# Value products of two attentions with 64 columns of one head, even and odd key blocks in the two column halves of TensorE

## The chip, the cores and the metric

The kernel runs on one core of one Trainium2 chip. A core has five engines with an instruction stream each: TensorE (PE in the profile, its weight loads PEld), VectorE (DVE), ScalarE (ACT), GpSimd (POOL) and SyncE (SP, which here only issues DMAs). They meet through semaphores. The working memory is SBUF; TensorE writes its products to PSUM, from which VectorE or ScalarE must take them. Both memories have 128 partitions. The metric is the device time of one execution in microseconds, the median of the runs.

## What is computed

One layer of a diffusion transformer for 512 latent positions and 256 context positions of width 1024. Four mixers work side by side on slices of one input projection, and their outputs are concatenated, projected by `w_out`, and passed to a mixture of 16 experts (two per position). The change touches the last product of two of the mixers, the differential attention (A) and the neighbourhood attention (B):

```python
# A: 4 heads, 2 x 32 query/key channels, 64 value channels, 768 keys (256 context + 512 latent)
s = jnp.einsum('bqhcd,bkhcd->bhcqk', q, k) * (A_QK ** -0.5)
p = jax.nn.softmax(s, axis=-1)
a = p[:, :, 0] - lam * p[:, :, 1]
o = jnp.einsum('bhqk,bkhd->bqhd', a, v)          # then an rms norm over the 64 channels of a head
# B: 4 heads of 64 channels, keys in a window of rows and columns, and the 256 context keys
p = jax.nn.softmax(jnp.concatenate([s_win, s_ctx], axis=-1), axis=-1)
ol = jnp.einsum('brqhik,brikhd->brqhd', p_win, v_rows) + jnp.einsum('brqhk,bkhd->brqhd', p_ctx, vc)
# afterwards
xl = xl + g1_l * (jnp.concatenate([a_l, b_l, p_l, h_l], axis=-1) @ lp['w_out'])
```

## The kernel before

The work goes through stages: modulation vectors (`ada`), the input projection in pieces, pool mixer and hyena convolution, then the two attentions, `w_out` with the residual (`xl`), the router, the experts, and a last norm. Each engine's instructions are ordered ahead of time by a scheduler that simulates the program; on the chip each engine keeps that order. A tile is taken from a pool under a tag with a fixed number of buffers, and an instruction that writes a new tile waits until the readers of the tile that had the buffer before are done.

Attention A (`attnA`) has 16 tiles of 128 queries, one for each of 4 heads and 4 query blocks. For a tile, TensorE makes two score rows `s` (L755, L756), VectorE takes each row's minimum (L773, scores have the opposite sign), ScalarE the exponentials `eA` (L774), and L783 and L784 join the two softmaxes. Two tiles later `outp` transposes the result on TensorE (`tA`, L801) and copies it to `aT` (L802), 6 key blocks of 128 by 256 queries for a pair of tiles. `av` then makes the value product for that head and pair (8 times in all): 6 matmuls with 128 value columns, which are those of two heads, accumulate into `poA` (L762), and ScalarE copies the 64 rows of the head that is wanted into `oA` (L764). After two heads a norm follows: `msA` (L815) on TensorE, and on VectorE four reciprocals L818, then L819 and L820.

The other generator, `projB` followed by `attnB`, is woven into A. `projB` makes the inputs of attention B (`pn` and `pl`, matmuls of L75 to L77: a product of values that are split in a high and a low part is three matmuls, and L71 and L72 make such a split, `wh` and `wl` for weights, `mix` for mixer outputs). It ends at about 301 us of the span, where the first scores `sB` of B are made. `attnB` has 16 tiles too, transposes `tB` (L993, copied to `eT` by L994), and 8 value products `poB`: 2 matmuls over 256 queries for the context (L1001) and 4 over 128 queries for the window (L1006), copied to `oB` by L1009. In the same stretch the modulation for the gate `g1` is made (`ad`, L416, with 32 columns), and the weights of `w_out` are multiplied by it (L452) and split (L71, L72). `w_out` itself is `pw` (L75 to L77), 24 halves of which L1047 adds to `xl`; the first two of four mixer groups come from B, so some of its matmuls stand among B's tiles and the rest behind.

The PSUM tag "x" has two buffers (`xbank`): in this stretch `tA`, `poA`, `msA` and `poB` and the columns of the modulation take turns in them. `tB` and `sB` use another tag.

```python
def xbank(name, shape=(128, 512)):
    return psx.tile(list(shape), F32, tag="x", name=name, bufs=2)
```

A float32 matmul appears as two instructions in the trace, and as one row in the order lists below; matmuls of split values (fp32r) are one in both.

Of the kernel before, what the change touches and what calls it, by code (L numbers as in the profile page):

```python
# [46 lines left out]
def tile_hybrid_block(ctx, tc, ins, out):  # L47
# [684 lines left out]

    LAG = 2

    def attnA():
        avs = aw([128, 6, 256], F32, "av")
        SY.dma_start(avs, avd.rearrange("(j p) c -> p j c", p=128))
        tiles = [(h, qt) for h in range(4) for qt in range(4)]
        qk, ss, st = {}, {}, {}
# [19 lines left out]
        def av(h, qp, aT):  # L759
            po = xbank("poA", (128, 256))  # L760
            for c in range(6):
                T.matmul(po, avs[:, c, (h // 2) * 128:(h // 2 + 1) * 128], aT[:, c, :], start=(c == 0), stop=(c == 5))  # L762
            rr = slice((h % 2) * 64, (h % 2) * 64 + 64)
            A.copy(st["os"][rr, qp * 256:(qp + 1) * 256], po[rr, :])  # L764

        def soft(ti, h, qt):
            if qt == 0 and h + 1 < 4:
# [141 lines left out]
    def attnB():  # L909
# [55 lines left out]
        for ti, (h, qt) in enumerate(tiles):  # L965
            if qt == LQ and h + 1 < 4:
                load_bias(h + 1)
            if ti == LT:
                load(1)
            if qt == 0 and h % 2 == 0:  # L970
                st["os"] = o1 if h == 0 else bw([128, 512], F32, "oB", 2)
            _, _, bv, bvx = ld[h // 2]
            bias = ld["b", h]
            p = sB.pop((h, qt))
            e = bw([128, 512], F32, "eB", NEB)
            ml = cst.tile([128, 4], F32, tag="ml", name="ml", bufs=6)
            V.tensor_sub(e[:, :256], p[:, :256], bias[:, qt, :])
            A.copy(e[:, 256:], p[:, 256:])
            V.tensor_reduce(ml[:, 0:1], e, axis=AX.X, op=ALU.min)
            A.activation(e, e, AF.Exp, scale=-1.0, bias=ml[:, 0:1], accum_out=ml[:, 1:2])  # L980
            V.reciprocal(ml[:, 1:2], ml[:, 1:2])
            A.activation(e, e, AF.Copy, scale=ml[:, 1:2])
            yield 1
            if ti + 2 < 16:
                scores(*tiles[ti + 2])
            yield 1
            qq = qt % 2
            if qq == 0:
                st["eT"] = e1 if ti == 0 else bw([128, 4, 256], F32, "eT", NET)
            eT = st["eT"]  # L990
            p = xbank("tB")
            for i in range(4):
                T.transpose(p[:, i * 128:(i + 1) * 128], e[:, i * 128:(i + 1) * 128], ident)  # L993
            (A.copy if ti % 2 else V.tensor_copy)(eT[:, :, qq * 128:qq * 128 + 128],  # L994
                                                  p.rearrange("p (c q) -> p c q", q=128))
            if qq == 1:
                yield 1
                qp = qt // 2
                po = xbank("poB", (128, 256))
                for i in range(2):  # L1000
                    T.matmul(po, bv[:, 4 + i, :], eT[:, 2 + i, :], start=(i == 0), stop=False)  # L1001
                for q2 in range(2):
                    qt_ = qp * 2 + q2
                    for i in range(2):
                        vv_ = bv[:, (0 if qt_ == 0 else 2) + i, :] if qt_ in (0, 3) else bvx[:, qt_ - 1 + i, :]
                        T.matmul(po[:, q2 * 128:(q2 + 1) * 128], vv_, eT[:, i, q2 * 128:(q2 + 1) * 128], start=False,  # L1006
                                 stop=(q2 == 1 and i == 1))
                rr = slice((h % 2) * 64, (h % 2) * 64 + 64)
                A.copy(st["os"][rr, qp * 256:(qp + 1) * 256], po[rr, :])  # L1009
            if qt == 3 and h % 2 == 1:  # L1010
                put_mix(None, 2 + h // 2, st["os"])
        flush()
# [981 lines left out]
```

## Time and profile before

| | |
|---|---|
| median of 3 runs | 752.04 us (747.57 to 754.37) |
| profiled execution | 753.25 us, of which 750.9 us are the span |
| mean granted TensorE clock in it | 0.945 of full speed |
| TensorE busy | 657.6 us (88%), 3886 matmul instructions |
| VectorE busy | 366.7 us (49%) |
| ScalarE busy | 245.4 us (33%) |

The span runs from the first to the last recorded instruction; 2.35 us lie around it. Busy shares are means over stages that are bound by different things, so the stretch in which the two attentions stand, from 240 to 421 us of the span, is read by itself. An instruction of TensorE overlaps the next in the trace, so the cost of one is read from the distance of two starts; the chain of waits gives such distances.

### The profile page before, as it was taken

The numbers are of one execution on the slowest core, as the hardware profiler recorded it, in microseconds if no ns is written. First come the engines' busy times: TensorE is split into PE (matmuls) and PEld (weight loads), VectorE is DVE, ScalarE is ACT, GpSimd is POOL, SyncE is SP. The second block draws the span as 40 slices with busy tenths as digits, with TensorE's granted clock in tenths as the row PEclk, the third lists the DMA queues.
The fourth block names the chain that finished last, engine by engine and source line by source line (L and its number), as shares of the span: only waits on it lengthen the run. The fifth ranks groups of instructions, "written<-read, shape, count | busy, mean of one in ns | idle before, by whom it ended". The sixth has DMA issues, their size and how long they took to land.

```text
span 750.9 us, 10264 instructions
## 1 busy us (share of the span) xinstructions
PE 657.6 (88%) x3886; PEld 421.5 (56%) x3886; DVE 366.7 (49%) x664; ACT 245.4 (33%) x421; POOL 145.0 (19%) x135
## 2 busy tenths in 40 slices
PE   3879999999879999689899947999999999976791
PEld 1457777879767796477788734444434445321230
DVE  3699835777816776994644673101111122211036
ACT  3573414341226774876831431000100001000024
POOL 1027433222205300000000351010211222111102
PEclk9969999999989999969999976999999999998995
DMA  8972357674483582595611675999789999999983
GB/s 318 417 260 110 127 189 263 267 263 159 152 219 140 172 273 71 175 389 195 244 57 57 239 281 214 413 412 406 276 282 321 375 405 376 407 394 399 394 314 116
DMA packets 46242, 197.81 MB, mean 263 GB/s; under 512 B 6330, under 2 KB 12961, under 8 KB 29290
## 3 DMA queue, kind: packets, MB, share of 16 engines
q1 hardware_dynamic: 38250, 175.55, 61.9%
q0 software_dynamic: 7056, 18.11, 8.4%
q10 hardware_dynamic: 880, 3.42, 1.1%
q8 instruction: 33, 0.54, 0.3%
q14 instruction: 23, 0.19, 0.1%
HBM read 177.79 MB, written 21.25 MB: 265 GB/s over the span
## 4 chain that ended last, share of the span: by engine, by line
PE 53%; DMA 10%; DVE 9%; ACT 4%; issue 3%; SPq 0%; POOL 0%; ACTq 0%; DVEq 0%; POOLq 0%
PE h L1449 16%; DMA mw<-in_moe_w_dram 8%; PE y L1516 7%; PE poA L762 3%; PE y L1502 2%; PE pw L75 2%; PE pw L76 2%; PE pw L77 2%; PE pn L76 2%; PE pn L77 1%; DMA qst<-qd 1%; PE pn L75 1%; DVE wl L72 1%; PE tpx L1413 1%; PE ad L416 1%
## 5 line engine op out<-in xcount | busy, mean ns | idle before, releaser
L1449 PE MATMUL h<-mw,xT 128*32 128x256 f32 (+2 forms) x928 | 154.7, 487 | 10.7 <-DMA mw<-in_moe_w_dram 10.6
L1449 PEld LDWEIGHTS h<-mw,xT 128*32 128x32 f32 (+2 forms) x928 | 55.9, 129 | 99.0 <-issue 66.7
L1464 ACT ACTIVATE hs<-h 64x512 f32<-64x512 f32 (+2 forms) x21 | 10.8, 512 | 195.7 <-PE h L1449 154.2
L1516 PE MATMUL y<-mw,hx 128*32 128x256 f32 (+2 forms) x432 | 70.1, 478 | 1.9 <-ACT hx L1476 0.7
L75 PE MATMUL pl<-ht,wh 128*128 128x512 f32 x128 | 52.6, 411 | 3.8 <-DVE bk L72 2.5
L77 PE MATMUL pl<-ht,wl 128*128 128x512 f32 x128 | 52.1, 407 | 0.0
L76 PE MATMUL pl<-ht,wh 128*128 128x512 f32 x128 | 52.0, 406 | 0.0
L1531 POOL DMA_INDIRECT xld<-ysb,r_ids x16 | 25.0, 1564 | 115.2 <-DVE ysb L1528 75.1
L1516 PEld LDWEIGHTS y<-mw,hx 128*32 128x32 f32 (+2 forms) x432 | 25.6, 127 | 34.4 <-issue 27.0
L1465 DVE SCALAR_TENSOR_TENSOR hs<-hs,r_gsl,h 64x512 f32<-64x512 f32 (+1 forms) x13 | 9.7, 744 | 67.0 <-ACT hs L1464 44.9
L72 DVE TENSOR_TENSOR wl<-raw,wh 128x2048 fp32r<-128x2048 f32 x14 | 33.4, 2388 | 13.9 <-ACT wh L71 13.9
L773 DVE TENSOR_REDUCE ml<-s 128x1 f32<-128x768 f32 x32 | 30.3, 948 | 12.7 <-PE s L756 12.6
L774 ACT ACTIVATE eA<-s,ml 128x768 f32<-128x768 f32 x32 | 28.8, 902 | 18.1 <-DVE ml L773 13.9
L71 ACT CAST wh<-raw 128x2048 fp32r<-128x2048 f32 x14 | 26.7, 1910 | 19.7 <-DMA raw<-in_w_in_dram 17.3
L75 PEld LDWEIGHTS pl<-ht,wh 128*128 128x128 f32 x128 | 24.6, 192 | 10.2 <-DVE bk L72 2.7
L1335 POOL DMA_INDIRECT xg<-hld,r_ids x12 | 12.2, 1015 | 85.3 <-PE tpx L1413 72.8
L762 PE MATMUL poA<-aT,av 128*128 128x256 f32 x96 | 26.8, 431 | 2.1 <-DVE aT L802 1.3
L76 PEld LDWEIGHTS pl<-ht,wh 128*128 128x128 f32 x128 | 24.5, 191 | 6.9 <-issue 1.6
L77 PEld LDWEIGHTS pl<-ht,wl 128*128 128x128 f32 x128 | 24.4, 191 | 6.4 <-issue 1.3
L1047 DVE TENSOR_TENSOR xl<-pw,xl 128x512 f32<-128x512 f32 x24 | 16.4, 688 | 20.3 <-PE pw L77 20.0
L75 PE MATMUL pw<-wh,mix 128*128 128x512 f32 x64 | 26.1, 407 | 0.0
L1414 DVE COPY xT<-tpx 128x512 f32<-128x512 f32 (+3 forms) x12 | 7.2, 602 | 37.9 <-PE tpx L1413 37.8
(453 smaller groups left out, 1419.2 us busy)
## 6 DMA issues: line engine op xcount, KB each, us to landing
mw<-in_moe_w_dram SPq DMA_DIRECT2D x92, 1024.0 KB
raw<-in_ada_dram SPq DMA_DIRECT2D x24, 1024.0 KB
raw<-in_w_in_dram SPq DMA_DIRECT2D x10, 1024.0 KB
raw<-in_w_out_dram SPq DMA_DIRECT2D x4, 1024.0 KB
mw<-in_moe_w_dram SPq DMA_DIRECT2D x6, 512.0 KB
mixd<-mx SPq DMA_DIRECT2D x5, 512.0 KB
kst<-kd SPq DMA_DIRECT2D x24, 96.0 KB
xin<-in_x_dram SPq DMA_DIRECT2D x4, 512.0 KB
```

Of the source, the lines that this page charges most:

```text
L71: A.copy(hi, src)
L72: (eng or V).tensor_sub(lo, src, f(hi))
L75: T.matmul(ps, a[0], b[0], start=start, stop=False)
L76: T.matmul(ps, a[0], b[1], start=False, stop=False)
L77: T.matmul(ps, a[1], b[0], start=False, stop=stop)
L762: T.matmul(po, avs[:, c, (h // 2) * 128:(h // 2 + 1) * 128], aT[:, c, :], start=(c == 0), stop=(c == 5))
L773: V.tensor_reduce(ml[:, cmp:cmp + 1], s[:, 0:768], axis=AX.X, op=ALU.min)
L774: A.activation(e[:, cmp, :], s[:, 0:768], AF.Exp, scale=-1.0, bias=ml[:, cmp:cmp + 1], accum_out=ml[:, 2 + cmp:3 + cmp])
L1047: V.tensor_add(xv, p, xv)
L1449: T.matmul(p, xk, b, start=(k == 0), stop=(k == 7))
L1516: T.matmul(p, x[k], b, start=(k == 0), stop=(k == 3))
L1531: G.indirect_dma_start(out=dst_, out_offset=bass.IndirectOffsetOnAxis(ap=at_, axis=0), in_=y, in_offset=None, bounds_check=last_, oob_is_e ...
```

## The change

Each value product uses only the 64 value columns of the head that is wanted. Even key blocks write partitions 0 to 63 of the PSUM tile, odd key blocks partitions 64 to 127, so that each half of the tile collects half of the sum. The number of matmuls is the same, each with 64 columns in place of 128. The halves are then added: a new function `halves_sum` lets ScalarE copy one half to the destination in SBUF, and VectorE adds the other half to it. In place of 16 copies of ScalarE there are 16 copies and 16 additions.

```diff
@@ -732,6 +732,13 @@
 
     LAG = 2
 
+    def halves_sum(dst, h, qp, po):
+
+        o = (h % 2) * 64
+        d = dst[o:o + 64, qp * 256:(qp + 1) * 256]
+        A.copy(d, po[64 - o:128 - o, :])
+        V.tensor_add(d, po[o:o + 64, :], d)
+
     def attnA():
         avs = aw([128, 6, 256], F32, "av")
         SY.dma_start(avs, avd.rearrange("(j p) c -> p j c", p=128))
@@ -759,9 +766,9 @@
         def av(h, qp, aT):
             po = xbank("poA", (128, 256))
             for c in range(6):
-                T.matmul(po, avs[:, c, (h // 2) * 128:(h // 2 + 1) * 128], aT[:, c, :], start=(c == 0), stop=(c == 5))
-            rr = slice((h % 2) * 64, (h % 2) * 64 + 64)
-            A.copy(st["os"][rr, qp * 256:(qp + 1) * 256], po[rr, :])
+                q = c % 2 * 64
+                T.matmul(po[q:q + 64], avs[:, c, h * 64:(h + 1) * 64], aT[:, c, :], start=(c < 2), stop=(c >= 4))
+            halves_sum(st["os"], h, qp, po)
 
         def soft(ti, h, qt):
             if qt == 0 and h + 1 < 4:
@@ -997,16 +1004,16 @@
                 yield 1
                 qp = qt // 2
                 po = xbank("poB", (128, 256))
+                hc = slice((h % 2) * 64, (h % 2) * 64 + 64)
                 for i in range(2):
-                    T.matmul(po, bv[:, 4 + i, :], eT[:, 2 + i, :], start=(i == 0), stop=False)
+                    T.matmul(po[i * 64:i * 64 + 64], bv[:, 4 + i, hc], eT[:, 2 + i, :], start=True, stop=False)
                 for q2 in range(2):
                     qt_ = qp * 2 + q2
                     for i in range(2):
-                        vv_ = bv[:, (0 if qt_ == 0 else 2) + i, :] if qt_ in (0, 3) else bvx[:, qt_ - 1 + i, :]
-                        T.matmul(po[:, q2 * 128:(q2 + 1) * 128], vv_, eT[:, i, q2 * 128:(q2 + 1) * 128], start=False,
-                                 stop=(q2 == 1 and i == 1))
-                rr = slice((h % 2) * 64, (h % 2) * 64 + 64)
-                A.copy(st["os"][rr, qp * 256:(qp + 1) * 256], po[rr, :])
+                        vv_ = bv[:, (0 if qt_ == 0 else 2) + i, hc] if qt_ in (0, 3) else bvx[:, qt_ - 1 + i, hc]
+                        T.matmul(po[i * 64:i * 64 + 64, q2 * 128:(q2 + 1) * 128], vv_, eT[:, i, q2 * 128:(q2 + 1) * 128],
+                                 start=False, stop=(q2 == 1))
+                halves_sum(st["os"], h, qp, po)
             if qt == 3 and h % 2 == 1:
                 put_mix(None, 2 + h // 2, st["os"])
         flush()
```

The lines behind the new function are 7 higher in the changed kernel: `s` is L762 and L763 there, `poA` L770, the row minimum L780, the join L791, `tA` L808, `msA` L822, `poB` L1009 and L1014; the new copy is L739 and the new addition L740.

The scheduler orders the engines anew, and the order moves at more places than the edited lines. TensorE at the first value product of A, before:

```order
L762 MATMUL poA<-aT,av 128x256 x6
L755 MATMUL s<-kst,qst 128x512
L756 MATMUL s<-kst,qst 128x256
L801 MATMUL tA<-ca,eA 128x128 x4
L755 MATMUL s<-kst,qst 128x512
L756 MATMUL s<-kst,qst 128x256
L75 MATMUL pn<-wh,ht_338 128x256 x2
L801 MATMUL tA<-ca,eA 128x128 x2
```

and in the changed kernel:

```order
L770 MATMUL poA<-aT,av 64x256 x6
L762 MATMUL s<-kst,qst 128x512
L763 MATMUL s<-kst,qst 128x256
L808 MATMUL tA<-ca,eA 128x128 x4
L762 MATMUL s<-kst,qst 128x512
L763 MATMUL s<-kst,qst 128x256
L75 MATMUL pn<-wh,ht_338 128x256 x2
L762 MATMUL s<-kst,qst 128x512
L763 MATMUL s<-kst,qst 128x256
```

The two transposes `tA`, which use the tag "x", stood before the last pair of scores here; they now stand behind it, behind 19 more `pn` and behind another pair of scores. VectorE at the same place, before:

```order
L773 TENSOR_REDUCE ml<-s 128x1
L72 TENSOR_TENSOR wl<-raw,wh 128x2048
L773 TENSOR_REDUCE ml<-s 128x1
L784 SCALAR_TENSOR_TENSOR eA<-eA,ml 128x768
L802 COPY aT<-tA 128x2x128
```

and in the changed kernel:

```order
L780 TENSOR_REDUCE ml<-s 128x1 x2
L72 TENSOR_TENSOR wl<-raw,wh 128x2048
L740 TENSOR_TENSOR oA<-poA,oA 64x256
L791 SCALAR_TENSOR_TENSOR eA<-eA,ml 128x768
L780 TENSOR_REDUCE ml<-s 128x1
```

The addition stands directly behind the split `wl` of a weight block; the row minimum that stood behind that split stands ahead of it now, and the copy `aT` has left this place.

TensorE at the end of the projection of B, where the last `pl` and the first scores `sB` stand; before (14 more `pl`, with one group of transposes among them, follow these rows, then `sB`):

```order
L75 MATMUL pl<-ht_338,wh 128x512
L755 MATMUL s<-kst,qst 128x512
L756 MATMUL s<-kst,qst 128x256
L76 MATMUL pl<-ht_340,wh 128x512
L815 MATMUL msA<-oA_2465,ca 128x512
L416 MATMUL ad_2516<-raw,sl_145 32x512
L755 MATMUL s<-kst,qst 128x512
L756 MATMUL s<-kst,qst 128x256
L416 MATMUL ad_2516<-raw,sl_145 32x512 x7
L77 MATMUL pl<-ht_338,wl 128x512
L75 MATMUL pl<-ht_338,wh 128x512
```

and in the changed kernel, from the last two `pl` on:

```order
L76 MATMUL pl<-ht_341,wh 128x512
L77 MATMUL pl<-ht_339,wl 128x512
L75 MATMUL sB<-bk_1994,bq_2756 128x256
L76 MATMUL sB<-bk_1994,bq_2756 128x256
L77 MATMUL sB<-bk_1994,bq_2756 128x256
L75 MATMUL sB<-bk_1994,bq_2756 128x256
L76 MATMUL sB<-bk_1994,bq_2756 128x256
L77 MATMUL sB<-bk_1994,bq_2756 128x256
L770 MATMUL poA<-aT,av 64x256 x3
L762 MATMUL s<-kst,qst 128x512
L763 MATMUL s<-kst,qst 128x256
L770 MATMUL poA<-aT,av 64x256
```

Of the 32 pairs of score rows of A, 24 stand before the last `pl` in the kernel before and 20 in the changed one; of the value products of A four and three; `msA` and the `ad` of the `g1` gate have moved behind the last `pl` (`msA` is 14 rows behind the last of these, and eight `ad` follow it).

TensorE at the last value product of B; before (13 more `pw` follow these rows, and then the six that use the last `oB`):

```order
L76 MATMUL pw<-wl,mix_2839 128x512
L1001 MATMUL poB<-eT,bv 128x256 x2
L1006 MATMUL poB<-eT,bvx 128x128 x2
L1006 MATMUL poB<-eT,bv 128x128 x2
L77 MATMUL pw<-wh,mix_2839 128x512
L75 MATMUL pw<-wh,mix_2838 128x512
L76 MATMUL pw<-wl,mix_2838 128x512
L77 MATMUL pw<-wh,mix_2838 128x512
L75 MATMUL pw<-wh,mix_2838 128x512
L76 MATMUL pw<-wl,mix_2838 128x512
```

and in the changed kernel:

```order
L77 MATMUL pw<-wh,mix_2845 128x512
L1009 MATMUL poB<-eT,bv 64x256 x2
L1014 MATMUL poB<-eT,bvx 64x128 x2
L1014 MATMUL poB<-eT,bv 64x128 x2
L75 MATMUL pw<-wh,mix_2845 128x512
L76 MATMUL pw<-wl,mix_2845 128x512
L75 MATMUL pw<-wh,mix_2845 128x512
L76 MATMUL pw<-wl,mix_2845 128x512
L77 MATMUL pw<-wh,mix_2845 128x512 x2
```

The `pw` that don't need the last `oB` stood behind the last value product and have moved before it; the six that do follow it directly. On VectorE the eight additions of B stand one to each value product, the last of them directly before the L72 that splits the last `oB`.

## Rows read from the trace of the kernel before

**Rows 1.** The page: shares of the chain that ended last, by engine.
```profile
PE 53%; DMA 10%; DVE 9%; ACT 4%; issue 3%; SPq 0%; POOL 0%; ACTq 0%; DVEq 0%; POOLq 0%
```

**Rows 2.** Windows: time, then PE, PEld, DVE, ACT, POOL busy, PEclk, DMA share, GB/s.
```profile
240.00:301.00 61.00, 58.39 (x358) 46.96 (x356) 43.87 (x68) 40.21 (x69) 10.96 (x7) 1.00 0.55 185
301.00:348.00 47.00, 37.46 (x174) 30.04 (x173) 38.72 (x63) 34.95 (x68) 0.77 (x1) 0.82 0.72 265
348.00:369.00 21.00, 18.01 (x117) 14.91 (x116) 13.15 (x28) 16.51 (x36) 0.00 (x0) 1.00 0.74 295
369.00:421.00 52.00, 52.00 (x263) 43.39 (x261) 23.75 (x38) 16.44 (x29) 0.00 (x0) 1.00 0.20 69
```

**Rows 3.** Timeline of PE at a value product of A (start, duration, instruction).
```profile
255.76 1.89 PE L762 MATMUL poA<-aT,av 128*128 128x256 f32 x8
...
258.70 0.60 PE L801 MATMUL tA<-ca,eA 128*128 128x128 f32 x4
```

**Rows 4.** Timeline of PE around matmuls with 32 columns.
```profile
261.57 0.28 PE L756 MATMUL s<-kst,qst 96*128 96x256 f32 x1
261.78 1.92 PE L416 MATMUL ad<-raw,sl 128*32 128x512 f32 x16
...
263.86 0.28 PE L76 MATMUL pn<-wl,ht 128*128 128x256 f32 x1
```

**Rows 5.** Timeline of PE in the experts: 64 and 128 columns.
```profile
577.01 3.65 PE L1516 MATMUL y<-mw,hx 128*64 128x512 f32 x16
...
583.76 3.70 PE L1516 MATMUL y<-mw,hx 128*128 128x512 f32 x8 [0.75 <-ACT hx L1476]
```

**Rows 6.** The chain of waits, 301 to 350 us (start, length, what).
```profile
304.60 2.20 DVE raw L452
...
321.23 5.33 PE poA L762 x12
...
337.18 4.00 PE poA L762 x12
...
345.74 2.59 PE poA L762 x12
348.33 0.86 PE poB L1001 x4
349.19 0.89 PE poB L1006 x8
```

**Rows 7.** DVE by line, 301 to 348 us: busy, mean ns, idle before.
```profile
L452 DVE TENSOR_TENSOR raw<-raw,g1b 128x2048 f32<-128x2048 f32 x4 | 9.1, 2282 | 1.9 <-issue 1.9
L773 DVE TENSOR_REDUCE ml<-s 128x1 f32<-128x768 f32 x8 | 7.5, 944 | 0.6 <-PE s L756 0.6
L784 DVE SCALAR_TENSOR_TENSOR eA<-eA,ml 128x768 f32<-128x768 f32 x5 | 5.0, 1008 | 0.1
...
L72 DVE TENSOR_TENSOR wl<-raw,wh 128x2048 fp32r<-128x2048 f32 x2 | 4.6, 2279 | 0.0
L802 DVE COPY aT<-tA 128x256 f32<-128x256 f32 x8 | 3.3, 413 | 4.0 <-PE tA L801 4.0
L977 DVE TENSOR_TENSOR eB<-sB,bias 128x256 f32<-128x256 f32 x7 | 2.8, 415 | 0.4 <-PE tB L993 0.4
```

**Rows 8.** DVE by line, 285 to 304 us.
```profile
L818 DVE RECIPROCAL oA<-oA 128x128 f32<-128x128 f32 x4 | 3.4, 909 | 0.9 <-ACT oA L816 0.9
```

**Rows 9.** Timeline at the last value product of B.
```profile
415.59 0.37 ACT L1009 COPY oB<-poB 64x256 f32<-64x256 f32 x1 [6.25 <-PE poB L1006]
...
415.99 0.63 ACT L71 CAST mix<-oB 128x512 fp32r<-128x512 f32 x1
...
416.65 0.69 DVE L72 TENSOR_TENSOR mix<-oB,mix 128x512 fp32r<-128x512 f32 x1
...
419.83 0.40 PE L75 MATMUL pw<-wh,mix 128*128 128x512 f32 x1
```

**Rows 10.** Windows in the experts, columns as in rows 2.
```profile
640.00:660.00 20.00, 19.35 (x210) 7.93 (x208) 4.50 (x11) 1.56 (x3) 3.11 (x2) 1.00 1.03 401
```

## The prediction

> **What bounds the kernel now.** The page comes first: TensorE makes 53% of the chain that ended last, VectorE 9% [rows 1]. That is a mean, so the stretch of the change is read next, in windows [rows 2]. From 240 to 301 us TensorE is busy for 58.4 of 61.0 us: the projection of B bounds it. From 301 to 348 us it is busy for 37.5 of 47.0 us, at a granted clock of 0.82, and VectorE for 38.7: here VectorE is the fullest engine. From 348 to 369 us it is mixed, and from 369 to 421 us TensorE has no gap at all. The chain shows how the second stretch is made: pieces of VectorE, such as the 2.20 us of L452, take turns with three value products of A, which take 5.33, 4.00 and 2.59 us for the same 12 instructions [rows 6]. The reader is to see two things: the same saved matmul time is worth all of itself in the first and last stretch, and in the second only where a value product is what VectorE waits for. Behind 421 us router and experts follow from the end of `w_out`, and where the experts run on the weights' DMAs there is no slack to give time back (TensorE 19.35 of 20 us, DMA share 1.03 [rows 10]); I let them move as one block.
>
> **The matmuls.** A value product of A takes 2.59 us [rows 6], 12 instructions of 0.216 us. Two instructions with 64 columns in the two halves run side by side: in the experts 16 with 64 columns take 3.65 us where 8 with 128 columns take 3.70 [rows 5]. So a product of A falls to 1.30 and saves 1.30, eight times 10.4 us. One of B takes 0.86 us for L1001 and 0.89 for the eight instructions of L1006, 1.75 together [rows 6]; halved it saves 0.87, eight times 7.0. Gross 17.4 us. What rows 5 leave open is the weight load: there 512 columns follow each load, here 256 and in L1006 only 128. For L1006 the bounds are therefore 0.44 and 0.89 as now; I take 0.44, from the only rows with 64 columns. With 0.89 the seven products of B on the path would give 3.1 us less.
>
> The Trainium skill, "TensorEngine Tiling (Array Packing)", section Tile-to-Partition Mapping (Restrictions), says that column tiling disables the fast weight load. That speaks against this change where few columns follow a load; no row here shows such a product, and by the rule alone the sum below would be at its upper bound for L1006.
>
> **Going in and out of column halves.** The 32-column `ad` shows what a visit costs. From the score matmul ahead of it to the second matmul behind it 2.29 us pass (261.57 to 263.86 [rows 4]). The work in it is 16 instructions of 512 columns, four side by side, as much as 8 of 256 full columns, 8 x 0.216 = 1.73, and two fp32r matmuls of 256 columns, 0.12 each. (A pair of score rows has 768 columns: 258.70 - 255.76 - 2.59 = 0.35 us [rows 3], 0.12 for 256.) That leaves 2.29 - 1.73 - 0.23 = 0.33 us for a visit. In the new order score rows split some products of A, so that there are 20 visits: 6.6 us. The bounds are nothing, if 64 columns behave as the 128-column visit of rows 3 that fits without a remainder, and 0.33. I take 0.33, since `ad` is the row of the same kind. Net on TensorE: 17.4 - 6.6 = 10.8 us.
>
> The Trainium skill, "TensorEngine Tiling (Array Packing)", section Tiling Modes (Key Properties), says that a change of the tiling mode drains TensorE. It gives no duration. The trace agrees, with the 0.33 us of rows 4; without such a cost the net would be the gross 17.4.
>
> **The copy and the addition.** ScalarE's copies stay 16, 0.37 us each [rows 9]. VectorE gets 16 additions. No row has a 64 x 256 one; the nearest is L977, PSUM and SBUF, 128 x 256: 0.415 us [rows 7]. As VectorE's time is by elements of a partition, I take 0.41 for each, 6.6 us in all, of which five fall into the second stretch (2.0 us), where VectorE is the fullest. The buffer of tag "x" is now held past the copy to the end of the addition, and that addition stands in VectorE's queue behind other work: at the first product of A behind a `wl` of 2.28 us [rows 7]. What needs the buffer are the next transposes `tA`; the scheduler has put them 23 rows later, behind scores and `pn`, so TensorE has work meanwhile. If that cover were gone, TensorE would wait for the `wl` and the addition, 2.7 us.
>
> **The first stretch, and what leaves it.** In the new order four pairs of score rows, one product of A, `ad`, `msA` and a few transposes have moved from before the last `pl` to behind it. By rows: 4 x 0.35 = 1.4, 2.6, 2.1 (rows 4 with its visit), some 0.9 for `msA` with two instructions of 512 columns (4 x 0.216), and 0.4: 7.4 us. The three products that stay save 3 x 1.30 = 3.9 and pay four visits, 1.3. The projection ends 7.4 + 2.6 = 10.0 us earlier.
>
> **The second stretch, and what comes into it.** Four pairs are two tiles of A. On VectorE a tile is two row minima (0.944 each), a join (1.008) and a copy (0.413) [rows 7], 3.3 us, twice 6.6. The reciprocals L818 of the first norm, which stood beside the projection, come along: 4 x 0.909 = 3.6 [rows 8]. With the five additions it is 12.2 us. That is the lower end, if the new work fills VectorE's gaps. The upper end goes by whole tiles: the stretch's 47.0 us less the four L452 (9.1) and two `wl` (4.6), which don't grow, for four tiles: 33.3 / 4 = 8.3 a tile, 16.7 for two. Against it stand the three products on the chain, 5.33 + 4.00 + 2.59 = 11.9, halved: 6.0. So A ends between 12.2 - 10.0 - 6.0 = -3.8 and 16.7 - 16.0 = +0.7. At the busy share that VectorE has there (38.72 / 47.0 = 0.82) the 12.2 become 14.9, which gives **-1.1**; I take that.
>
> The Trainium skill, "TensorEngine Tiling (Array Packing)", section Performance Considerations (PSUM Bottleneck), warns that tiling speeds TensorE and not the emptying of PSUM. It speaks for the upper end; by it alone the sum of this stretch would be +0.7. The trace so far agrees as far as VectorE's 0.82 goes.
>
> **The third and the last stretch.** A product of B on the chain saves 0.87 - 0.33 = 0.54. Three stand on it before 369 us, -1.6, and four behind, where TensorE has no gap, -2.2. At the last one cover is lost. Before, 19 `pw` followed it on TensorE, up to 419.83 us; in that time copy, cast and split of `oB` (415.59, 415.99, 416.65 [rows 9]) were done. In the new order these `pw` stand ahead of the product and the six that need `oB` directly behind it. TensorE waits for copy 0.37, addition 0.41, cast 0.63 and their hand-offs, 0.1 each: **+1.7**. The low part (L72) comes while four matmuls that don't need it run.
>
> **Sum.** -1.1 - 1.6 - 2.2 + 1.7 = -3.2 us on the profiled execution's 753.25, which is 1.21 above the median: 750.05 there, **749.0** as a median to be measured. From the bounds of A (-2.7 and +1.8 about the value taken), of L1006 (+3.1) and of the visits (eleven are counted, four in the first stretch and seven later, -3.6) its own range is 743 to 754.
>
> **Rivals.**
> *The saving passes through.* If the chain's VectorE pieces move along because nothing of the moved work is late, the end moves by TensorE's net 10.8: 742.5, as a median 741. For it: products of A stand on the chain at up to 5.33 us, and the last stretch is all TensorE. Against: VectorE at 82% gets 12.2 us more. Chance 0.25.
>
> *The softmax tail is bare: slower.* The two tiles that have moved behind the projection run with nothing beside them, VectorE bound by its addition behind each; the products, already half as long, no longer are what it waits for. Then the 6.0 us don't come off: 16.7 - 10.0 = +6.7, with -2.1 behind it +4.6, 757.9 or as a median 757; and if the lower clock of this stretch (0.82) holds for a product's length more (5.33 against 2.59, +2.7), 759 to 760. It decides from the point where VectorE has no idle time before a product's `aT` copy; L802 still has 4.0 us of it, all for the transposes [rows 7], which speaks against. Chance 0.19.
>
> *The halves don't run side by side.* Then a product costs as much as before and the visits and the wait at the end come on top, 6.6 + 1.7 = 8.3: 760 as a median. Against it stands rows 5 with the same pattern in the same kernel. Chance 0.05.
>
> **How the numbers follow.** The forecast has the remaining 0.51. About 1%, 7.5 us, is what a measurement of this kernel can tell from no change: below 744.5 is faster, above 759.6 slower. Faster has the first rival, 0.25, less a little that stops short, plus what of the forecast has cheap visits: 0.25. Slower has the third rival and the part of the second with the lower clock: 0.13. The rest, 0.62, is within. The range reaches from the first rival's 741, a us lower for visits at nothing, to the second's end, 740 to 760.
>
> **What the new profile would show.** A product of A as 12 instructions in about 1.3 us, of B in about 0.87, and 0.33 us lost around each (right), or 2.59 and 1.75 (third rival). The first `sB` at about 291 us in place of 301. The last product of A ending about 1 us earlier than 348.3, or later, and in the stretch before it VectorE's share above 0.85 with additions on the chain (second rival). A gap of TensorE of 1.7 us before the last six `pw` of the first half. The prediction is wrong above all if the moved tiles run beside something else than I think, or if another wait on tag "x" opens, which would show as idle time of PE with the addition as its releaser.

## The result: slower by 1.4%

The changed kernel takes 765.03 us (median of four, 764.52 to 765.61), the kernel before 753.2 us in the same comparison (747.57 to 755.56); the ratio is 1.0143, 95% interval 1.0109 to 1.0176. The forecast was 749.0 us, the range 740 to 760. The profiled execution takes 764.69 us with a span of 762.9 us, 12.0 us more than before, at a mean granted clock of 0.921 in place of 0.945.

Where the 12.0 us arise is read from the first and last starts in the tile views, at the same five marks in each trace (us of the span; the last `poA` is its last instruction):

| | before | changed | longer by |
|---|---|---|---|
| first `poA` | 241.7 | 242.0 | 0.3 |
| first `poA` to first `sB` (the projection ends) | 59.5 | 56.7 | -2.8 |
| first `sB` to last `poA` | 46.8 | 59.3 | +12.5 |
| last `poA` to first `tH` (end of `w_out`'s first half) | 73.9 | 73.9 | 0.0 |
| first `tH` to the end of the span | 329.0 | 331.0 | +2.0 |

The windows of the changed kernel are cut at its own marks (columns as in [rows 2]):

```profile
240.00:299.00 59.00, 52.56 (x320) 42.10 (x319) 36.98 (x58) 34.67 (x60) 10.64 (x7) 0.91 0.50 171
299.00:358.00 59.00, 44.42 (x212) 27.00 (x212) 49.45 (x81) 42.45 (x77) 0.77 (x1) 0.77 0.61 222
358.00:379.00 21.00, 18.74 (x115) 13.65 (x111) 15.61 (x32) 16.67 (x34) 0.00 (x0) 0.76 0.82 325
379.00:431.00 52.00, 50.43 (x268) 39.69 (x266) 26.02 (x44) 16.65 (x31) 0.00 (x0) 1.00 0.15 50
```

The granted clock is below 1.00 in three of the four stretches, where before only the second had 0.82 [rows 2]. VectorE's work in the second is 49.45 us, before 38.72.

The chain of waits of the changed kernel, the products that answer to [rows 6] (start, length, what):

```profile
348.38 2.76 PE poA L770 x12
...
356.97 1.45 PE poA L770 x12
358.42 0.43 PE poB L1009 x4
358.85 0.44 PE poB L1014 x8
```

At the full clock a product of A takes 1.45 us with its entry and one of B 0.43 + 0.44; the halves run side by side, and L1014 with 128 columns for each load is halved too. But one of the two products of A shown here runs at 1.2 GHz and takes 2.76 us.

TensorE's timeline at the first product of A:

```profile
242.03 1.74 PE L770 MATMUL poA<-aT,av 128*64 128x256 f32 x12 [0.78 <-ACT aT L809]
...
245.60 0.50 PE L75 MATMUL pn<-wh,ht 128*128 128x256 f32 x2 [0.48 <-ACT wh L71]
247.85 0.50 PE L762 MATMUL s<-kst,qst 96*128 96x512 f32 x1 [1.75 <-ACT eA L781]
248.19 0.28 PE L763 MATMUL s<-kst,qst 96*128 96x256 f32 x1
250.02 0.58 PE L76 MATMUL pn<-wl,ht 128*128 128x256 f32 x1 [1.55 <-DVE wl L72]
250.40 0.42 PE L77 MATMUL pn<-wh,ht 128*128 128x256 f32 x1
250.62 0.41 PE L75 MATMUL pn<-wh,ht 128*128 128x256 f32 x1
```

The reader sees three waits (0.48, 1.75 and 1.55 us) and then `pn` at a distance of 0.21 us in place of 0.12: the same matmuls at 1.2 GHz, after these waits, until 256 us. In the kernel before, the waits at this place are 0.59, 0.45 and 0.31 us and the `pn` behind them come at 0.12:

```profile
246.52 0.44 PE L801 MATMUL tA<-ca,eA 128*128 128x128 f32 x2 [0.59 <-ACT oA L764]
247.41 0.50 PE L755 MATMUL s<-kst,qst 96*128 96x512 f32 x1 [0.45 <-ACT eA L774]
...
248.34 0.38 PE L76 MATMUL pn<-wl,ht 128*128 128x256 f32 x1 [0.31 <-DVE wl L72]
248.56 0.28 PE L77 MATMUL pn<-wh,ht 128*128 128x256 f32 x1
248.68 0.28 PE L75 MATMUL pn<-wh,ht 128*128 128x256 f32 x1
```

In the whole first stretch the view of waits gives 6.4 us in the changed kernel and 2.6 before. From the start of the first product (241.69 us before) to the `pn` that waits for `wl` it is 7.99 us in place of 6.65. VectorE starts that `wl` 0.66 us later behind the product, since one more row minimum stands ahead of it, and takes 0.68 us longer over it. The split `wl` of the kernel before, and that of the changed one with the instruction of GpSimd during which it starts:

```profile
245.82 2.47 DVE L72 TENSOR_TENSOR wl<-raw,wh 128x2048 fp32r<-128x2048 f32 x1
```

```profile
246.55 1.26 POOL L890 TENSOR_TENSOR smm<-s,icn 64x512 f32<-64x512 f32 x1
...
246.82 3.15 DVE L72 TENSOR_TENSOR wl<-raw,wh 128x2048 fp32r<-128x2048 f32 x1
```

Between 299 and 358.4 us a `wl` takes 2.28 us; what GpSimd does to such instructions of VectorE is seen more plainly in e11 below.

VectorE by line in the second stretch (299 to 358.4 us), the lines that answer to [rows 7] and [rows 8], and the additions:

```profile
L780 DVE TENSOR_REDUCE ml<-s 128x1 f32<-128x768 f32 x12 | 11.4, 947 | 1.9 <-PE s L763 1.9
L791 DVE SCALAR_TENSOR_TENSOR eA<-eA,ml 128x768 f32<-128x768 f32 x7 | 7.1, 1010 | 0.9 <-ACT eA L790 0.8
L825 DVE RECIPROCAL oA<-oA 128x128 f32<-128x128 f32 x4 | 3.4, 908 | 1.0 <-ACT oA L823 1.0
L740 DVE TENSOR_TENSOR oA<-poA,oA 64x256 f32<-64x256 f32 x4 | 1.7, 421 | 0.5 <-ACT oA L739 0.5
```

Four row minima, two joins, four reciprocals and four additions have come in, as the order said; the fifth addition lies behind the mark.

At the last product of B the wait of 1.57 us answers to the step on the lost cover; before, the same copy and cast were done beside `pw` [rows 9] (timeline of PE):

```profile
427.76 0.39 PE L1014 MATMUL poB<-eT,bv 128*64 128x128 f32 x4
429.72 0.50 PE L75 MATMUL pw<-wh,mix 128*128 128x512 f32 x1 [1.57 <-ACT mix L71]
```

### The profile page after: what moved, and what is told of

The parts are those of the page before. It is cut to its first block, busy times and chain, and to the rows that moved or that the text cites. A ratio compares the mean times of both kernels' runs of the same rounds, so it can differ in the third digit from the quotient of the medians.

```text
span 762.9 us, 10277 instructions
## 1 busy us (share of the span) xinstructions
PE 659.8 (86%) x3886; PEld 409.9 (54%) x3886; DVE 376.3 (49%) x680; ACT 247.6 (32%) x421; POOL 143.8 (19%) x135
## 4 chain that ended last, share of the span: by engine, by line
PE 28%; DMA 16%; DVE 5%; ACT 3%; issue 1%; POOL 0%; SPq 0%; ACTq 0%; DVEq 0%; POOLq 0%
DMA mw<-in_moe_w_dram 16%; PE h L1456 11%; PE y L1523 5%; PE y L1509 2%; PE pw L75 2%; PE pw L76 2%; PE pw L77 2%; PE tB L1000 1%; PE tpx L1420 1%; DVE hl L1146 1%; PE sB L75 1%; PE poA L770 1%; PE poB L1009 1%; PE tph L1481 1%; DMA xg<-hld,r_ids 1%
## 5 line engine op out<-in xcount | busy, mean ns | idle before, releaser
L1456 PEld LDWEIGHTS h<-mw,xT 128*32 128x32 f32 (+2 forms) x928 | 56.3, 129 | 96.5 <-issue 68.8
L1523 PE MATMUL y<-mw,hx 128*32 128x256 f32 (+2 forms) x432 | 72.2, 489 | 4.3 <-DMA mw<-in_moe_w_dram 3.4
L72 DVE TENSOR_TENSOR wl<-raw,wh 128x2048 fp32r<-128x2048 f32 x14 | 34.1, 2438 | 14.2 <-ACT wh L71 14.2
L780 DVE TENSOR_REDUCE ml<-s 128x1 f32<-128x768 f32 x32 | 30.2, 950 | 15.1 <-PE s L763 15.1
L71 ACT CAST wh<-raw 128x2048 fp32r<-128x2048 f32 x14 | 26.7, 1906 | 21.0 <-DMA raw<-in_w_in_dram 16.7
L762 PE MATMUL s<-kst,qst 96*128 96x512 f32 x32 | 16.4, 513 | 15.2 <-ACT eA L781 8.9
L1342 POOL DMA_INDIRECT xg<-hld,r_ids x12 | 12.2, 1018 | 86.4 <-PE tpx L1420 72.9
L76 PE MATMUL pw<-wl,mix 128*128 128x512 f32 x64 | 25.4, 397 | 0.0
```

Of the source, the lines that this page charges most:

```text
L71: A.copy(hi, src)
L72: (eng or V).tensor_sub(lo, src, f(hi))
L76: T.matmul(ps, a[0], b[1], start=False, stop=False)
L762: T.matmul(s[:, 0:512], q, ks[:, cmp, 0:512], start=True, stop=True)
L780: V.tensor_reduce(ml[:, cmp:cmp + 1], s[:, 0:768], axis=AX.X, op=ALU.min)
L1456: T.matmul(p, xk, b, start=(k == 0), stop=(k == 7))
```

## Experiments

Each kernel is compared with the kernel before on the same chip. For some, TensorE, VectorE and ScalarE are held to a given order between the first scores of A and the first half of `w_out`: every instruction there gets an ordering edge, without a semaphore, to the one that stands before it in that order. The additions of e1, e6, e13, e16 and e17 are left out of this and stand where the scheduler puts them. Such kernels call the engines through a recording helper, so that the recorded instructions have its line, L62, in the profile and are told apart by their tiles.

```python
for eng_, text in ORDERS.items():           # text: places in program order, as steps
    at, prev = 0, None
    for word in text.split():
        step, _, times = word.partition("*")
        for _ in range(int(times or 1)):
            at += int(step)
            if prev is not None:
                behind(logs[eng_][at], prev, False)
            prev = logs[eng_][at]
```

### Order, matmuls and addition taken apart (e1 to e7)

**e1_before_order**: all of the change, held to the order of before.

> All of the change, but TensorE, VectorE and ScalarE keep the order of the kernel before from the first scores of A to the first half of w_out; the 16 additions stand where the scheduler then puts them. Theory O (the new order costs the time: two softmax tiles and the reciprocals moved behind the projection, the cover at the end gone): faster than before, 742 to 749, the projection ends before 300 us. Theory C (shorter products leave TensorE idle ahead of VectorE and its granted clock falls, in any order): 755 to 766, with a granted clock below 1.0 between 240 and 301 us. Theory S (the addition on VectorE and the longer hold of the PSUM buffer cost it): 758 to 766.

Measured: 752.74 us, ratio 0.998 (0.9949 to 1.001). The loss of the change is gone, but there is no gain either: the time lies between the ranges of the three theories.

**e2_full_copyadd**: the matmuls of before, emptied as in the change.

```diff
-            A.copy(st["os"][rr, qp * 256:(qp + 1) * 256], po[rr, :])
+            d = st["os"][rr, qp * 256:(qp + 1) * 256]
+            A.activation(d, po[rr, :], AF.Copy, scale=0.0)
+            V.tensor_add(d, po[rr, :], d)
```

> The value products of before, with 128 columns, but emptied as in the change: ScalarE writes (with a factor of zero) the destination and VectorE adds the 64 rows to it. The scheduler's order is then like that of the change (20 pairs of score rows ahead of the last pl, six pw behind the last product). Theory O: 760 to 768, all of the loss without any column halves. Theory C: 751 to 756. Theory S: 760 to 768 as well (told from O by the first kernel).

Measured: 767.72 us, 1.0176 (1.0115 to 1.0237). Without any column halves the kernel is as slow as the change: it is the way of emptying PSUM that makes the scheduler choose an order of this kind (20 pairs of score rows ahead of the last `pl`, six `pw` behind the last product of B). It is not the same order in every row.

**e3_no_sum** and **e7_no_sum_before_order**: halves, but no addition; e7 is held to the order of before, e3 has the scheduler's own, which is like it (24 pairs ahead of the last `pl`).

```diff
         A.copy(d, po[64 - o:128 - o, :])
-        V.tensor_add(d, po[o:o + 64, :], d)
```

> The change without the addition: ScalarE copies one half, the other half of the key blocks is left out of the output. The order is then like that of before (24 pairs ahead of the last pl). Theory O: faster, 740 to 747, by the 17.4 us of halved products less the visits. Theory C: 755 to 765, clock below 1.0 from 240 to 301 us. Theory S: 740 to 747.

> The column halves with one copy (the other half of the key blocks is left out of the output), in the order of before: the halved products alone. If the halved matmul time passes through where TensorE has no gap: 742 to 747. Theory C (what they save is waited away ahead of VectorE and the granted clock falls in the gaps): 750 to 755, with the clock below 1.0 between 250 and 260 us and at 0.5 to 0.7 up to 370 us, as in e3_no_sum.

Measured: e3 754.4 us, 1.0001 (0.997 to 1.0032); e7 750.45 us, 0.9948 (0.9897 to 0.9998). Of 17.4 us of matmul time the halves alone give 0 to 5.

**e4_one_half**: 64 columns, all in one half, one copy.

```diff
-                q = c % 2 * 64
-                T.matmul(po[q:q + 64], avs[:, c, h * 64:(h + 1) * 64], aT[:, c, :], start=(c < 2), stop=(c >= 4))
+                q = h % 2 * 64
+                T.matmul(po[q:q + 64], avs[:, c, h * 64:(h + 1) * 64], aT[:, c, :], start=(c == 0), stop=(c == 5))
-            halves_sum(st["os"], h, qp, po)
+            rr = slice(q, q + 64)
+            A.copy(st["os"][rr, qp * 256:(qp + 1) * 256], po[rr, :])
```

(The product of B is edited likewise.)

> 64 columns of the one head, but all key blocks into the one column half, one copy, no addition; the order is like that of before. If the halves run side by side only as a pair: a product of A takes 2.6 us as before, and with 18 visits of 0.33 us the time is 753 to 760. If 64 columns alone are already half the time: 740 to 747.

Measured: 760.59 us, 1.0088 (1.0061 to 1.0115). The timeline of PE has the same 12 instructions, with 64 columns, at the length of the full product, where the change has 1.74 (242.03, above):

```profile
241.96 2.80 PE L770 MATMUL poA<-aT,av 128*64 128x256 f32 x12 [0.78 <-ACT aT L810]
```

So only the pair runs side by side, and the rival that the halves don't is out.

**e5_after_order**: the instructions of before (128 columns, one copy, no addition), held to the order of the change.

> The instructions of the kernel before, with 128 columns and one copy and no addition, in the order that TensorE, VectorE and ScalarE have in the changed kernel from the first scores of A to the first half of w_out. Theory O (the order alone is the loss): 763 to 768, like the change. Theory H (the order costs only because VectorE has the additions and tag x is held): 752 to 757.

Measured: 768.87 us, 1.0198 (1.0148 to 1.0249). The order alone costs as much as the whole change (1.0143, with an interval that overlaps this one). Its windows, cut at its own marks:

```profile
239.00:296.00 57.00, 52.22 (x311) 44.41 (x312) 34.41 (x52) 32.92 (x57) 8.99 (x6) 0.94 0.50 169
296.00:357.00 61.00, 47.94 (x210) 35.52 (x210) 48.36 (x77) 41.93 (x77) 0.77 (x1) 0.80 0.60 220
```

The projection takes 56.3 us from the first product and the stretch behind it 61.8, 15.0 more than before.

**e6_full_copyadd_before_order**: e2 held to the order of before.

> 128 columns, copy and addition as in e2_full_copyadd, in the order of before. Theory O: the addition and the longer hold cost little, 754 to 758, with TensorE waiting some 3.5 us for the first addition, 1.3 less than the 4.7 us of e1_before_order, since the product is longer. Theory S (addition and hold are the loss): 764 to 770.

Measured: 756.66 us, 1.0029 (0.9982 to 1.0075). TensorE waits 4.8 us for the first addition, not 3.5. The addition starts 8.45 us behind the start of the first product in e1 and in e6; what the longer product fills is another wait of e1, 0.57 us for `wh`.

Put together, as ratios to the kernel before:

| | order of before | order of the change (e2: of its kind) |
|---|---|---|
| 128 columns, copy | 1 | 1.0198 (e5) |
| 128 columns, copy and addition | 1.0029 (e6) | 1.0176 (e2) |
| halves, copy | 0.9948 (e7) | not run |
| halves, copy and addition | 0.998 (e1) | 1.0143 (the change) |

Read across, the order costs 1.5 to 2%, which is clear of the intervals. Read down a column, the halves give some 0.3 to 0.5% and the addition costs about 0.3% in the order of before; these are no larger than the intervals.

### Where in the order (e9, e10, e13)

> Only attention A is changed (halves, copy, addition); B as before. The order around the projection is that of the change (20 pairs of score rows ahead of the last pl). Theory O: the loss is in A's part of the order, 762 to 768. If the end of B (cover of the last product gone) carried half of the loss: 756 to 761.

> Only attention B is changed; A as before, with the order around the projection of before (24 pairs). Theory O, loss in A's part: 751 to 756 (eight products 0.54 us shorter, 1.7 us waited at the end). If the end of B carried half of the loss: 757 to 761.

> Only attention B changed (halves, copy, addition), in the order of before, so that the cover of the last product stays. By the steps of the prediction: eight products 0.54 us shorter and nothing waited at the end, 4 us below before, 749 to 752. If the lower clock takes it back: 753 to 757.

Measured: e9 (A alone) 767.13 us, 1.0169 (1.0107 to 1.023); e10 (B alone) 751.62 us, 0.9964 (0.9939 to 0.9989); e13 753.01 us, 0.9983 (0.9959 to 1.0007). The loss is A's. B alone gains a little, and holding its order (e13) adds nothing to that. Both have A's instructions of before up to the end of the projection, and waits at the place shown above that together are no longer than before (e10: 0.51, 0.45 and 0.37 us). Yet `pn` is at the distance of 1.2 GHz from 249.6 to 253.0 us in e10, and the projection takes 61.0 us from the first product in each, 1.5 more than in the one trace of before. From 250 to 260 us in e10:

```profile
250.00:260.00 10.00, 10.00 (x61) 9.22 (x61) 5.51 (x12) 6.14 (x11) 1.88 (x1) 0.85 0.36 126
```

So the clock can fall here in kernels in which A is as before. The timeline of PE in e13 shows where B's gain goes there:

```profile
367.19 1.12 PE L62 MATMUL poB<-eT,bv 128*64 128x256 f32 x4 [0.86 <-ACT eT L62]
...
381.84 0.87 PE L62 MATMUL poB<-eT,bv 128*64 128x256 f32 x8
...
393.23 0.65 PE L62 MATMUL poB<-eT,bv 128*64 128x256 f32 x4
```

From one product to the next in the gapless stretch 393.23 - 381.84 = 11.39 us pass; before it is 11.98 at this place (377.39 to 389.37). That is 0.59 us for a product, as worked out (0.54). But from 367.19 to 381.84 it is 14.65 us against 11.67: the product at 367.19 stands in a stretch at the lower clock (1.12 us for L1009 as against 0.65), and so do the `w_out` matmuls behind it (granted clock 0.73 from 370 to 380 us, before 1.00). One such stretch takes back the gain of five products. That the halves bring it on is not shown: in the 21 us behind the last product of A the granted clock is 0.94 in e11 and 0.95 in e14 (both below), which have 128 columns.

### What bounds the stretch behind the projection (e11, e12, e14, e15, e8)

**e11** and **e12**: L452 on GpSimd, in the kernel before and with halves that are summed as in e8 below.

```diff
-            V.tensor_tensor(t, t, g, op=ALU.mult)
+            G.tensor_tensor(t, t, g, op=ALU.mult)
```

> The kernel before, with the four products of the w_out weights with g1 (L452, 4 x 2.28 us of VectorE between 301 and 348 us) on GpSimd, which is idle there. If VectorE bounds that stretch, as the account of the loss says: 744 to 749. If TensorE or ScalarE does: 752 to 757.

> The column halves with two copies of ScalarE and the sum on GpSimd, and the products with g1 on GpSimd too, so that VectorE has less to do than before and none of the additions. If VectorE's load is what kept the halved matmuls from paying: 738 to 746, below e11_gate_on_gpsimd by 4 or more. If the lower clock takes it back anyway: like e11_gate_on_gpsimd.

Measured: 757.79 us, 1.0052 (1.0026 to 1.0078), and 759.63 us, 1.0064 (1.0032 to 1.0097): e11 is slower, which its expectation did not allow for, and e12 is like it. The timeline of e11, VectorE and GpSimd:

```profile
314.10 6.07 POOL L452 TENSOR_TENSOR raw<-raw,g1b 128x2048 f32<-128x2048 f32 x1 [7.12 <-DMA raw<-in_w_out_dram]
...
316.06 0.95 DVE L773 TENSOR_REDUCE ml<-s 128x1 f32<-128x768 f32 x1
...
316.93 4.06 DVE L784 SCALAR_TENSOR_TENSOR eA<-eA,ml 128x768 f32<-128x768 f32 x1
...
320.91 4.53 POOL L452 TENSOR_TENSOR raw<-raw,g1b 128x2048 f32<-128x2048 f32 x1
...
321.91 3.55 DVE L780 TENSOR_TENSOR ml<-ml,lr 128x1 f32<-128x1 f32 x1
```

While GpSimd works at its 128 x 2048 product, VectorE's join takes 4.06 us in place of 1.0 [rows 7], and a product of 128 x 1 elements 3.55 in place of 0.15; the one ends 0.8 us behind GpSimd's instruction, the other with it. The row minimum at 316.06 us, which reads PSUM, keeps its 0.95. The split `wl` that had begun ahead of GpSimd's product keeps its 2.28 us. The load came back to VectorE as waiting inside its instructions, so this pair says nothing on who bounds the stretch.

**e14** and **e15** take L452 away without giving it to another engine (one column of it is left).

> The kernel before in its own order, the four products of the w_out weights with g1 (L452, 9.1 us of VectorE) left out but for one column, so the gate is missing in the output. If VectorE bounds 301 to 348 us: 744 to 748. If not: 752 to 755.

> The changed kernel in its own order, the same four products left out but for one column. If VectorE bounds the longer stretch there: 755 to 758, 7 to 9 us below the change. If not: 762 to 766.

Measured: 1769.79 and 1779.43 us. Without the gate the residual sends the positions to other experts, and the branch for crowded experts runs; of these two only what lies ahead of the router can be read. From first `sB` to last `poA` e14 takes 43.4 us, 3.4 less than before, though VectorE is busy for 8.1 us less (30.66 in place of 38.72); e15 takes 59.9, not less than the change (59.3), with 7.7 us less of VectorE (42.09 in place of 49.75) and a granted clock of 0.69 in place of 0.77, and from the first to the last `poA` 114.6 against 116.0. So VectorE's load is not the bound by itself. What the stretch costs goes by the round of a tile through four steps (scores, minimum, exponentials, transposes), each waiting for another engine; that is argued from the waits of TensorE in it (in the changed kernel 5.8 us for exponentials, 2.6 for the join, 2.0 for `aT`) and was not tried by itself.

**e8_pool_add_before_order**: ScalarE copies both halves, GpSimd adds.

```diff
+        t = cst.tile([128, 256], F32, tag="hv", name="hv", bufs=2)
         A.copy(d, po[64 - o:128 - o, :])
-        V.tensor_add(d, po[o:o + 64, :], d)
+        rawA.copy(t[o:o + 64, :], po[o:o + 64, :])
+        G.tensor_add(d, t[o:o + 64, :], d)
```

> The whole sum, but ScalarE takes both halves out of PSUM (two copies) and GpSimd adds them in SBUF, in the order of before: no addition on VectorE, and tag x is free after the second copy. If the hold behind VectorE was what kept e1_before_order at the time of before: 744 to 749. Theory C: 750 to 755, like e7_no_sum_before_order.

Measured: 753.59 us, 0.9983 (0.9925 to 1.0042), no difference to be told from e1 or from before. (`rawA` is ScalarE without the held order.)

### The gap and the clock (e16 to e18)

e16 and e17 are one kernel: e1 with 28 redundant matmuls in the gap of TensorE ahead of the first addition. The scheduler then puts that addition two rows further ahead on VectorE, directly behind `wl`; e18 has it there too, without the fill.

```diff
-            T.matmul(s[:, 512:768], q, ks[:, cmp, 512:768], start=True, stop=True)
+            last_s = T.matmul(s[:, 512:768], q, ks[:, cmp, 512:768], start=True, stop=True)
+            if (h, qt, cmp) == (1, 0, 1):
+                fill.append(last_s)
+                for _ in range(28):
+                    fill.append(rawT.matmul(s[:, 768:1024], q, ks[:, cmp, 0:256], start=True, stop=True))
```

(The instructions in `fill` get ordering edges of their own, behind this pair of scores.)

> Kernel of e1_before_order with 28 more matmuls of 256 columns (some 3.3 us, into unused columns of a score tile) in the gap of TensorE ahead of the first addition. Theory C, that idle time lowers the clock: the granted clock of 250 to 260 us rises from 0.81 to 0.95 or more, and the projection ends as early as in e1_before_order or up to 2 us earlier, counted from the first product (62.6 us), in spite of 3.3 us more work. If the clock falls for another reason: 0.8, and the same end.

> The kernel of e16_gap_filled, timed: halves, sum and order of before, with 28 redundant matmuls in the gap ahead of the first addition. By its one look, 749.9: 747 to 751, 3 to 6 us below before; if that look was a fortunate one, 751 to 754.

> As e1_before_order, with the first addition directly behind wl on VectorE, as it stands in e16_gap_filled, and no fill. Theory C (the clock falls in the gap): TensorE still waits some 3 us, the clock of 240 to 260 us stays below 0.95, the projection takes 60 to 61.5 us from the first product, and the time is 1 to 3 us above e17_gap_filled_timed. If the earlier addition was all: clock 1.00, 58 to 59 us, and the time of e17_gap_filled_timed.

Measured: e16 749.88 us in its one execution; e17 749.66 us, 0.9938 (0.9913 to 0.9964); e18 753.31 us, 0.9981 (0.9952 to 1.001). The gap in e1, by the timeline of PE:

```profile
244.22 0.51 PE L62 MATMUL pn<-wh,ht 128*128 128x256 f32 x2 [0.57 <-ACT wh L62]
249.47 0.69 PE L62 MATMUL tA<-ca,eA 128*128 128x128 f32 x2 [4.75 <-DVE oA L760]
...
250.60 0.41 PE L62 MATMUL pn<-wl,ht 128*128 128x256 f32 x1
250.81 0.63 PE L62 MATMUL pn<-wh,ht 128*128 128x256 f32 x2
```

In e18 the same wait is 2.85 us. The fill in e17:

```profile
244.69 3.51 PE L788 MATMUL s<-kst,qst 96*128 96x256 f32 x28
```

And the windows from 240 to 260 us of e1, of e18 and of e17, in this order:

```profile
240.00:260.00 20.00, 14.12 (x88) 11.60 (x90) 13.97 (x21) 11.76 (x21) 9.84 (x6) 0.83 0.58 191
```

```profile
240.00:260.00 20.00, 15.81 (x101) 12.60 (x101) 15.25 (x24) 13.81 (x24) 11.59 (x7) 0.91 0.64 215
```

```profile
240.00:260.00 20.00, 18.90 (x139) 15.35 (x138) 16.29 (x26) 14.72 (x25) 11.20 (x7) 1.00 0.62 211
```

From the first product to the end of the projection e1 takes 62.6 us, e18 60.3 and e17 58.7. The earlier addition is worth 2.3 of it, the fill 1.6: 3.5 us of work that nobody needs makes the stretch shorter, with TensorE's granted clock at 1.00 through it (0.91 without, 0.83 in e1; e16, the other execution of this kernel, has 1.00 and 58.7 us too). e17 has the lowest median here. Its 3.65 us on e18 rest on twelve executions of each (746.84 to 751.17 and 748.46 to 755.85); the two that were traced end alike, with spans of 748.2 and 748.3 us, since e17 takes 2.3 us more between the last `poA` and the first `tH` (75.4 against 73.1).

## Why the prediction was wrong

Between the forecast (-3.2 us on the profiled execution) and the 12.0 us by which the span grew lie 15.2 us: 7.2 at the end of the projection, 3.6 in the stretch behind it (+12.5 where 14.9 - 6.0 = +8.9 stood), 2.1 in the part of B, 2.0 behind `tH` and 0.3 ahead of the first product. (The recorded sum, 750.05 - 1.21, is 748.8 where 749.0 stands; nothing hangs on it.)

**The projection ends 10.0 us earlier: this step failed.** The work did leave (7.4 us) and the products were shorter, but the end came only 2.8 us earlier; with the order alone and 128 columns (e5) 3.2 in place of 7.4. I took the stretch as bound by TensorE throughout. At its start, from 240 to 250 us, it is VectorE that is full (9.97 of 10 us in the changed kernel, 9.85 before), TensorE waits for `wl` and for the exponentials, so that work that moves away, and the part of a product that is saved, leave a longer wait there. The waits are 3.8 us longer; `wl`, which the last of the three is for, is done 1.34 us later behind the start of the first product, by the new order and by GpSimd. Then comes the clock: from 250.02 to 255.95 us the matmuls run at 1.2 GHz, and of these 5.93 us some 2.6 are lost (`pn` 0.213 us apart in place of 0.118). Both together make 6.4 of the missing 7.2. That filling the gap keeps the clock up is shown in the order of before, by e17 against e18; in the order of the change it was not tried. And since the clock falls in e10 and e13 behind waits that together are no longer than before, how much of the 2.6 us is due to the change stays open. The Trainium skill, "TensorE: Matmul & The Clock Gate", section HAM oscillation — how this bites in real kernels, warns of idle gaps between bursts of matmuls; the trace agrees, with the lower clock behind the three waits at 242 to 250 us.

**The stretch behind it.** Its growth without the halves, worked out as 14.9 (taken) to 16.7 us (by whole tiles), was right: with 128 columns it was 15.0 without the additions (e5) and 16.9 with them (e2). VectorE's added work is 10.7 us by the windows (49.45 against 38.72), 12.2 was worked out. The 6.0 us of the halved products were mis-sized. The products did get some 5 us shorter: in e7 the three take 2.76, 2.76 and 1.35 us to the next matmul, where [rows 6] has 5.33, 4.00 and 2.59. But the stretch lost only 2.4 in the order of before (46.8 to 44.4 in e1 and e7) and 2.5 in that of the change (61.8 in e5 to 59.3, with the additions come in). In e7 one of the three, with 2.76 us, is still on the chain of waits; in place of the others something else ends last. The granted clock fell as well (0.70 in e7 from 298 to 343 us, before 0.82), and what that takes back was not measured by itself. So the sum for A is 12.5 - 2.8 = +9.7 where -1.1 stood.

**B and the end.** A product of B saves 0.59 us where TensorE has no gap, and the wait at the end is 1.57 us: the prices of 0.54 and 1.7 were right. The sum, -2.1, is 0.0. With 128 columns in the order of the change (e5) it is 77.5 us from the last `poA` to the first `tH`, 3.6 more than before: that is what the order costs here, where only the 1.7 of the one wait stood. The halves give 3.6 back, near the 3.8 of seven products at 0.54. The granted clock from 358 to 379 us is 0.76, where the kernel before had 1.00 and e5 has 0.95 behind its last `poA`; its share was not measured by itself.

**Visits and loads.** From 242.03 to 243.71 us a product with its exit takes 1.68 us, 0.38 more than 1.30; 0.33 was taken. L1014's 0.44 us chooses the lower of the two bounds. By the Trainium skill, "TensorEngine Tiling (Array Packing)", section Tile-to-Partition Mapping (Restrictions), the fast weight load is off in column tiling; no cost of that is seen here, even where only 128 columns follow a load: a load for `poA` with 64 columns takes 137 ns (median), one with 128 columns before 190. Whether these float32 loads were fast ones before no run here tells.

**The rivals.** The bare softmax tail came nearest, with the upper price of the two tiles; it was put at 757 because the 10.0 us were set against it. Its mechanism, VectorE as the bound, is not borne out: VectorE's share is 0.84 (49.45 of 59 us), where above 0.85 was its sign, and with 7.7 us less of VectorE's work (e15) the stretch is no shorter. What makes the scheduler go there is the addition on VectorE: e2, with 128 columns and the addition, gets an order of the same kind, while e3 and e4, with one copy, and e12, with two copies and the sum on GpSimd, keep 24 pairs of score rows ahead of the last `pl`, as before. The 2.0 us behind `tH` were in no step. In single profiled executions that part is 1.9 to 2.8 us longer than before in e2, e5 and e9 too, and -1.1 to +3.0 in the kernels with the order of before around the projection; its cause stays open.

## What to carry to other kernels

Before a saving on an engine is counted, look in windows of some 10 us, not of 50, at whether that engine waits there: time saved ahead of a wait is waited away. On TensorE a gap can cost more than its own length: in the changed kernel and in e1, e5, e6 and e18 the matmuls behind it run at 1.2 GHz for some 3.5 to 6 us. And where a scheduler orders the engines, one more instruction of VectorE between a product and the release of its buffer can move other work by tens of rows: hold the old order with ordering edges and measure that first.

## What was not expected of the hardware

Redundant matmuls in a gap made a kernel faster (e17 0.9938, e18 without them 0.9981). GpSimd's product over 128 x 2048 elements in SBUF held up those of VectorE's instructions that start during it with two tensors in SBUF, however small, until it ended: 3.55 us for 128 x 1 elements in place of 0.15 (e11). The same pattern stands in the changed kernel at the first product of A, where `wl` takes 3.15 us. The Trainium skill, "GPSIMD Engine Reference", section 1. Specifications, names this contention without a size; the trace of e11 agrees, and gives one.
